# Transposing x as fp32 words that hold two bf16 each: four PE transposes a tile in place of eight

## The chip, the cores and the metric

The kernel runs on one core of a Trainium2 chip. The metric is the device time of one execution in microseconds (us), the median of repeated runs. PE is the tensor engine, PEld its weight loads, DVE the vector engine, ACT the scalar engine, POOL the GpSimd engine, SP the engine that issues the DMA transfers. A run has a state, fast or slow, judged by its time and its granted clock. On one chip the runs of the kernel before lie within 0.25% of each other. The kernel before had medians of 211.32, 211.36 and 211.38 us on three occasions and of 211.68 us on a fourth; the last three of these are on record for three different chips. So runs are compared with the kernel before of the same occasion.

## The reference

```python
batch, m, k, n = 16, 512, 1024, 768      # x: (16, 512, 1024), weight: (1024, 768), all float32
def reference(x, weight, bias, residual):
    return (np.matmul(x, weight) + bias + residual).astype(np.float32)
```

That is 8192 rows, in 64 tiles of 128. The kernel must read x (33.6 MB), the residual (25.2 MB) and the weight (3.1 MB) and write the output (25.2 MB): 87 MB.

## The kernel before

Rows are handled in groups of eight tiles (`J = 8`): one transfer brings x of a group, one its residual, one takes its output away. For each tile ACT casts x to bf16, PE transposes it into PSUM in eight pieces of 128x128, DVE copies these to SBUF, PE multiplies with the bf16 weight into PSUM, and DVE and POOL add residual and bias in place. Element pairs (2i, 2i+1) of a row of x share a place `i`: the weight is laid out to match (`w_d`), and each transpose takes the even or the odd elements of a block.

```python
n_c = K // (2 * P)                                              # 4 blocks of 256 elements
steps = [(c, e) for c in range(n_c) for e in range(2)]          # block, even or odd
w_d = weight.rearrange("(c p e) n -> p c e n", p=P, e=2)
# ... (loads, stores and rings of buffers cut: x_sb 2 groups, ro 4 groups, xb 4, xt 4, pt 2 tiles)
def cast(t, engine="act"):
    if t < n_t:
        xb[t] = ring(sb, "xb", t, 4, [P, n_c, P, 2], BF16)
        copy = nc.scalar.copy if engine == "act" else nc.vector.tensor_copy
        K_(copy(out=xb[t].rearrange("p c i e -> p (c i e)"), in_=x_sb[t // J][:, t % J, :]))

def transp(t):
    if t < n_t:
        pt = ring(ps, "pt", t, 2, [P, len(steps), P], BF16)
        for i, (c, e) in enumerate(steps):
            K_(nc.tensor.transpose(out=pt[:, i, :], in_=xb[t][:, c, :, e], identity=ident))
        xt[t] = ring(sb, "xt", t, 4, [P, len(steps), P], BF16)
        K_(nc.vector.tensor_copy(out=xt[t], in_=pt))

def mm(t, i, n0, nl):                                           # two chunks: 512 and 256 columns
    c, e = steps[i]
    K_(nc.tensor.matmul(po[t][:, n0:n0 + nl], lhsT=xt[t][:, i, :], rhs=w_sb[:, c, e, n0:n0 + nl],
                        start=(i == 0), stop=(i == len(steps) - 1)))
# ... (start cut)
for t in range(HEAD, n_t):
    cast(t + 2)
    S, j = divmod(t, J)
    if (t + 2) % J == J - 1:
        # ... (the first group's loads come in halves)
        load_x(S + X_BUFS)
        load_res(S + X_BUFS)
        if 1 <= S < n_s - 1:
            store(S - 1)
    if t < n_t - 1:
        for i in range(len(steps)):
            mms(t, i)                                           # both chunks of step i
            # ...
            if i == T_STEP:
                transp(t + 1)                                   # the next tile's transposes
    # ... (residual and bias, last stores)
```

## Time and profile before

| | kernel before |
|---|---|
| time, median | 211.28 us (211.23 to 211.34, the first three runs) |
| PE busy | 202.7 us, 97% of the profiled span of 210.0 us |
| one tile on PE, steady | 3.05 us: 16 output matmuls 2.60, 8 transposes 0.45 |
| moved by DMA | 87.27 MB |

From the page of the kernel before: the busy times, three of the rows in which the span is cut in 40 slices (tenths of busy time; the last is GB/s moved), and the chain of waits.

```profile
PE 202.7 (97%) x1555; PEld 131.7 (63%) x1555; DVE 104.9 (50%) x139; ACT 67.6 (32%) x68; POOL 115.1 (55%) x71
...
PE   7999999999999999999999999999999999999980
...
DMA  6999999999999999999999999999999999999993
GB/s 235 428 422 425 432 419 423 421 428 432 417 485 404 420 445 410 434 449 404 439 449 428 421 412 435 449 412 429 425 412 460 434 409 445 420 417 432 417 395 151
...
PE 96%; DVE 1%; issue 0%
PE po L101 79%; PE pt L95 14%; PE po L169 3%; PE po L189 1%; DVE xt L97 0%; DVE ro L128 0%; DVE warm L155 0%
```

Two things are full at once, PE and DMA, and the chain names only one of them.

The groups of instructions of the kernel before that the change touches (busy us, mean ns of one, idle time before them and what ended it):

```profile
L97 DVE COPY xt<-pt 128x1024 bf16<-128x1024 bf16 x64 | 44.1, 691 | 87.7 <-PE pt L95 87.5
...
L95 PEld LDWEIGHTS <-xb 128*128 128x128 bf16 x512 | 34.2, 99 | 8.8 <-DVE xb L87 0.7
L95 PE MATMUL pt<-ident,xb 128*128 128x128 bf16 x512 | 39.2, 220 | 0.0
```

The ends of matmuls are modelled, so 220 ns is not what one costs. What it costs is the distance between starts. The timeline of PE in the kernel before (start us, length us):

```profile
102.06 0.61 PE L95 MATMUL pt<-ident,xb 128*128 128x128 bf16 x8
102.51 2.76 PE L101 MATMUL po<-w_sb,xt 128*128 128x512 bf16 x16
105.11 0.39 PE L95 MATMUL pt<-ident,xb 128*128 128x128 bf16 x4
```

Eight transposes hold PE from 102.06 to 102.51, 0.45 us or 56 ns each, and sixteen output matmuls from 102.51 to 105.11, 2.60 us.

Stretches of the span of the kernel before (busy us and count of each engine, then the granted PE clock, the DMA share, GB/s):

```profile
20.00:60.00 40.00, 40.00 (x321) 26.51 (x319) 20.31 (x26) 13.88 (x15) 31.39 (x18) 1.00 1.01 424
...
100.00:140.00 40.00, 40.00 (x316) 26.42 (x315) 20.61 (x28) 13.92 (x14) 24.68 (x14) 1.00 1.01 432
```

PE does not wait at all, and the DMA share is at 1.01. The Trainium skill ("Perfetto Trace Analysis", Roofline) gives about 435 GB/s as what the 16 DMA engines of a core reach together; the trace agrees, with 424 to 432 GB/s at a full share over stretches of 40 us (single slices of the page swing from 395 to 485).

### The profile page before, as it was taken

Reading aid. Unit: us, or ns where it says so; the run is one execution under the profiler, and the core shown is the slowest. Engines: PE = TensorE matmul, PEld = TensorE weight load, DVE = VectorE, ACT = ScalarE, POOL = GpSimd, SP = SyncE. Lnnn points to the kernel's source line nnn. Section 1 sums busy time; section 2 is a strip of 40 time slices with the busy share of each in tenths; the row PEclk is TensorE's granted clock in tenths of the full one; section 3 lists DMA queues with packets and bytes.
Section 4 is the critical chain, followed back from the end, with each engine's and each line's share of the span. In section 5 each row is a group of like instructions: output and inputs, shape, how many; then the busy total and the mean of one; then the engine's idle time right before and its main releaser. Section 6 shows DMA issues by size and latency. Waiting matters only on the chain.

```text
span 210.0 us, 3632 instructions
## 1 busy us (share of the span) xinstructions
PE 202.7 (97%) x1555; PEld 131.7 (63%) x1555; DVE 104.9 (50%) x139; ACT 67.6 (32%) x68; POOL 115.1 (55%) x71
## 2 busy tenths in 40 slices
PE   7999999999999999999999999999999999999980
PEld 2666666666666666666666666666666666666650
DVE  0646464455445545544554455455445545545650
ACT  2543315331533063313432053230623116330000
POOL 2000097979999505991099703993039930799000
PEclk9999999999999999999999999999999999999998
DMA  6999999999999999999999999999999999999993
GB/s 235 428 422 425 432 419 423 421 428 432 417 485 404 420 445 410 434 449 404 439 449 428 421 412 435 449 412 429 425 412 460 434 409 445 420 417 432 417 395 151
DMA packets 6211, 87.27 MB, mean 416 GB/s; under 512 B 690, under 2 KB 818, under 8 KB 2099
## 3 DMA queue, kind: packets, MB, share of 16 engines
q1 hardware_dynamic: 6192, 87.03, 97.7%
q8 instruction: 12, 0.20, 0.4%
q14 instruction: 5, 0.03, 0.0%
q10 hardware_dynamic: 2, 0.00, 0.0%
HBM read 61.87 MB, written 25.17 MB: 415 GB/s over the span
## 4 chain that ended last, share of the span: by engine, by line
PE 96%; DVE 1%; issue 0%
PE po L101 79%; PE pt L95 14%; PE po L169 3%; PE po L189 1%; DVE xt L97 0%; DVE ro L128 0%; DVE warm L155 0%
## 5 line engine op out<-in xcount | busy, mean ns | idle before, releaser
L101 PE MATMUL po<-w_sb,xt 128*128 128x256 bf16 (+1 forms) x1024 | 176.7, 326 | 0.1
L101 PEld LDWEIGHTS <-xt 128*128 128x128 bf16 x1024 | 97.6, 98 | 58.8 <-DVE xt L97 0.5
L118 POOL TENSOR_TENSOR ro<-ro,bias_sb 128x768 f32<-128x768 f32 x52 | 92.4, 1813 | 51.7 <-DMA ro<-in_residual_dram 41.7
L87 ACT CAST xb<-x_tile 128x1024 bf16<-128x1024 f32 x62 | 62.8, 1044 | 115.5 <-DMA x_tile<-in_x_dram 54.2
L97 DVE COPY xt<-pt 128x1024 bf16<-128x1024 bf16 x64 | 44.1, 691 | 87.7 <-PE pt L95 87.5
L128 DVE TENSOR_TENSOR ro<-po,ro 128x768 f32<-128x768 f32 (+2 forms) x53 | 49.3, 933 | 2.9 <-PE po L101 2.8
L95 PEld LDWEIGHTS <-xb 128*128 128x128 bf16 x512 | 34.2, 99 | 8.8 <-DVE xb L87 0.7
L95 PE MATMUL pt<-ident,xb 128*128 128x128 bf16 x512 | 39.2, 220 | 0.0
L118 POOL TENSOR_TENSOR ro<-ro,tmp 128x768 f32<-128x768 f32 x12 | 21.5, 1815 | 26.6 <-DMA ro<-in_residual_dram 25.3
L126 DVE TENSOR_TENSOR tmp<-po,bias_sb 128x768 f32<-128x768 f32 x12 | 11.4, 948 | 0.9 <-POOL ro L118 0.5
L169 PE MATMUL po<-warm 128*128 128x512 bf16 x15 | 6.1, 581 | 1.2 <-DVE warm L155 1.2
L175 ACT CAST w_sb<-ro 128x768 bf16<-128x768 f32 x4 | 3.3, 832 | 4.0 <-DMA ro<-in_weight_dram 4.0
L169 PEld LDWEIGHTS <-warm 128*128 128x128 bf16 x15 | 1.9, 136 | 4.0 <-issue 2.7
L87 DVE CAST xb<-x_tile 128x1024 bf16<-128x1024 f32 x2 | 1.4, 693 | 4.9 <-DMA x_tile<-in_x_dram 4.9
L177 DVE CAST w_sb<-ro 128x768 bf16<-128x768 f32 x4 | 2.2, 554 | 2.2 <-DMA ro<-in_weight_dram 2.2
L160 ACT ACT_TABLE_LOAD x1 | 1.3, 1283 | 2.0 <-POOL ident masks.py:199 2.0
L189 PE MATMUL po<-tmp 128*128 128x512 f32 (+1 forms) x4 | 1.5, 500 | 0.0
L197 DVE COPY bias_sb<-po 128x768 f32<-128x768 f32 x1 | 1.0, 957 | 0.2 <-PE po L189 0.2
L189 PEld LDWEIGHTS po<-tmp 128*128 128x128 f32 x4 | 0.7, 190 | 0.5 <-issue 0.5
L132 POOL MEMSET tmp<- 128x768 f32 x1 | 0.7, 737 | 0.3 <-POOLq L266 0.3
L155 DVE MEMSET warm<- 128x256 uint32 x1 | 0.3, 272 | 0.9 <-PEq L266 0.9
masks.py:199 POOL TENSOR_SCALAR_AFFINE_SELECT ident<-ident 128x128 bf16<-128x128 bf16 x1 | 0.3, 292 | 0.1
(8 smaller groups left out, 1.0 us busy)
## 6 DMA issues: line engine op xcount, KB each, us to landing
out_dram<-ro SPq DMA_DIRECT2D x7, 3072.0 KB, 23.9
x_tile<-in_x_dram SPq DMA_DIRECT2D x5, 4096.0 KB, 30.5
ro<-in_residual_dram SPq DMA_DIRECT2D x5, 3072.0 KB, 17.8
ro<-in_residual_dram SPq DMA_DIRECT2D x6, 1536.0 KB, 27.4
x_tile<-in_x_dram SPq DMA_DIRECT2D x3, 2048.0 KB, 25.8
x_tile<-in_x_dram SPq DMA_DIRECT2D x5, 1024.0 KB, 18.5
ro<-in_weight_dram SPq DMA_DIRECT2D x4, 768.0 KB, 9.0
out_dram<-ro SPq DMA_DIRECT2D x1, 1536.0 KB, 11.6
```

The costliest lines, as they stand in the source:

```text
L87: K_(copy(out=xb[t].rearrange("p c i e -> p (c i e)"), in_=x_sb[t // J][:, t % J, :]))
L95: K_(nc.tensor.transpose(out=pt[:, i, :], in_=xb[t][:, c, :, e], identity=ident))
L97: K_(nc.vector.tensor_copy(out=xt[t], in_=pt))
L101: K_(nc.tensor.matmul(po[t][:, n0:n0 + nl], lhsT=xt[t][:, i, :], rhs=w_sb[:, c, e, n0:n0 + nl], start=(i == 0), stop=(i == len(steps) - 1),))
L118: K_(nc.gpsimd.tensor_add(out=r, in0=r, in1=tmp[t] if t < EARLY else bias_sb))
L126: K_(nc.vector.tensor_add(out=tmp[t], in0=p, in1=bias_sb))
L128: K_(nc.vector.tensor_add(out=row(t, n0, nl), in0=p, in1=row(t, n0, nl)))
L160: K_(nc.scalar.copy(out=warm_a, in_=warm_a))
L169: K_(nc.tensor.matmul(warm_ps[:, 0:512], lhsT=warm[:, 0:P], rhs=warm, start=True, stop=True))
L175: K_(nc.scalar.copy(out=w_sb[:, c, e, :], in_=w_st[:, c, e, :]))
L177: K_(nc.vector.tensor_copy(out=w_sb[:, c, e, :], in_=w_st[:, c, e, :]))
L189: K_(nc.tensor.matmul(bias_ps[:, n0:n0 + nl], lhsT=ones, rhs=bias_row[:, n0:n0 + nl], start=True, stop=True,))
```

## The change

Two neighbouring bf16 of a row are 32 bits. The change transposes them as one fp32 word: four transposes of 128 words in place of eight of 128 bf16, in the hope of fewer PE instructions. After the transpose a word still holds the even element and the odd one; the output matmuls pick theirs with a step of two when they load weights.

```diff
     def cast(t, engine="act"):
...
-            xb[t] = ring(sb, "xb", t, 4, [P, n_c, P, 2], BF16)
+            xb[t] = ring(sb, "xb", t, 4, [P, K], BF16)
...
     def transp(t):
         if t < n_t:
-            pt = ring(ps, "pt", t, 2, [P, len(steps), P], BF16)
-            for i, (c, e) in enumerate(steps):
-                K_(nc.tensor.transpose(out=pt[:, i, :], in_=xb[t][:, c, :, e], identity=ident))
-            xt[t] = ring(sb, "xt", t, 4, [P, len(steps), P], BF16)
+            pt = ring(ps, "pt", t, 2, [P, n_c, P], FP32)
+            pairs = xb[t][:, :].bitcast(FP32)
+            for c in range(n_c):
+                K_(nc.tensor.transpose(
+                    out=pt[:, c, :], in_=pairs[:, c * P:(c + 1) * P], identity=ident
+                ))
+            xt[t] = ring(sb, "xt", t, 4, [P, n_c, P], FP32)
             K_(nc.vector.tensor_copy(out=xt[t], in_=pt))
 
     def mm(t, i, n0, nl):
         c, e = steps[i]
+        both = xt[t][:, c, :].bitcast(BF16).rearrange("p (m e) -> p e m", e=2)
         K_(nc.tensor.matmul(
-            po[t][:, n0:n0 + nl], lhsT=xt[t][:, i, :], rhs=w_sb[:, c, e, n0:n0 + nl],
+            po[t][:, n0:n0 + nl], lhsT=both[:, e, :], rhs=w_sb[:, c, e, n0:n0 + nl],
...
-    ident = const.tile([P, P], BF16, name="ident")
+    ident = const.tile([P, P], FP32, name="ident")
```

More of the change, by code (lines that the diff above doesn't have):

```diff
@@ L84, in cast @@
         if t < n_t:
-            xb[t] = ring(sb, "xb", t, 4, [P, n_c, P, 2], BF16)
+            xb[t] = ring(sb, "xb", t, 4, [P, K], BF16)
             copy = nc.scalar.copy if engine == "act" else nc.vector.tensor_copy
-            K_(copy(
-                out=xb[t].rearrange("p c i e -> p (c i e)"), in_=x_sb[t // J][:, t % J, :]
-            ))
+            K_(copy(out=xb[t], in_=x_sb[t // J][:, t % J, :]))
     def transp(t):
         if t < n_t:
-            pt = ring(ps, "pt", t, 2, [P, len(steps), P], BF16)
-            for i, (c, e) in enumerate(steps):
-                K_(nc.tensor.transpose(out=pt[:, i, :], in_=xb[t][:, c, :, e], identity=ident))
-            xt[t] = ring(sb, "xt", t, 4, [P, len(steps), P], BF16)
+            pt = ring(ps, "pt", t, 2, [P, n_c, P], FP32)
[5 more added lines that the diff above has]
+            xt[t] = ring(sb, "xt", t, 4, [P, n_c, P], FP32)
             K_(nc.vector.tensor_copy(out=xt[t], in_=pt))
```

## The prediction

> **What bounds the kernel now.** Two things at once. The chain of waits is 96% PE: 79% output matmuls, 14% transposes of x. In the steady part a tile takes 3.05 us: sixteen matmuls 2.60 us, eight bf16 transposes 0.45 us (56 ns from start to start); PE never waits from 20 to 200 us (windows). But DMA is as full: share 1.00 to 1.01, at 424 to 432 GB/s, for 87.27 MB that the change does not touch. A group of eight tiles moves 10.5 MB in 24.4 us, which is 430 GB/s. The casts already find x late once per group (ACT waits 6.2 to 7.7 us for x); only the ring of four cast tiles hides that from PE.
>
> **What the change does.** Per tile, eight weight loads and matmuls of 128 bf16 columns become four of 128 fp32 columns. PSUM and xt bytes stay. The copy out of PSUM becomes 512 fp32 words in place of 1024 bf16 (0.69 us); fp32 additions out of PSUM took 691 ns at 512 columns, so I estimate 0.69 us again. The output matmuls load weights at a step of two elements; the transposes of before do that already, at 99 ns against 98 ns packed: no cost.
>
> **The uncertain term: one fp32 transpose.** The fp32 bias matmuls are the only sample: each is split in two instructions, and 768 columns took 1.35 us to the start of the next matmul: 1.76 ns a column, four times bf16. At that price four transposes take 0.90 us, and the kernel is 29 us slower. But the Trainium skill ("TensorE: Matmul & The Clock Gate", Terms) says that the transpose mode is 4x faster for FP32, so I expect one instruction at bf16's rate; no run here shows it. The weight load then matters: the same page (Fast Weight Load) excludes fp32 from the fast load. The trace agrees in direction: 190 ns for an fp32 load, 98 ns for bf16. I estimate 110 ns a transpose, load-bound: the 92 ns more, plus some 15 to 25 ns. Four take about 0.44 us against 0.45 now: PE gains almost nothing. If the loads hide, four take 0.23 us and PE is freed of 14 us.
>
> **Critical path.** Even then little shows, since DMA is full: only the tail (200 to 210 us: 2.57 MB, about 6 us of work at the full rate) can shrink, by 2 to 3 us; PE would wait for x at group starts instead. So halved transposes yield about 208 us, a neutral cost 210 to 211, 190 ns each (loads not hidden) about 231, four-fold columns 240.
>
> **Prediction: 210.4 us**, 8 in 10 between 207.5 and 216. Faster by over 2%: 4%; within 2%: 76%; slower by over 2%: 20%.
>
> **What would show each step.** Groups of instructions: 256 fp32 transposes, and the distance between two (110 ns expected; 56: loads hidden; 190 or more: wrong). Copy xt 0.69 us. Windows: output matmuls still 2.60 us a tile, DMA share still 1.00. If transposes got cheap, PE waits for casts, these for x, at group starts, and the span still ends at about 87 MB over 430 GB/s plus start and tail.
>
> **What would make it wrong.** fp32 transposes split into several passes; a switch cost between fp32 and bf16 on PE; strided loads of xt that slow the output matmuls (16 ns on each adds 16 us); or transfers faster than 430 GB/s once PE frees buffers earlier.

## The result

The changed kernel took 211.29 us (median of six runs, 211.19 to 211.48), the kernel before 211.32 us (six runs, 211.23 to 211.53): ratio 0.9998, 95% interval 0.9985 to 1.0011. A ratio here is the mean time of one kernel's fast runs over that of the other's of the same rounds, so it is not quite the ratio of the medians. The forecast was 210.4 us, 0.9 us (0.4%) less than before. The measured time lies inside the range that was given, but the gain did not come: the interval allows 0.3 us of it at most. The changed kernel's result is right.

From the page of the changed kernel:

```profile
PE 200.6 (96%) x1274; PEld 130.6 (62%) x1299; DVE 105.0 (50%) x139; ACT 67.6 (32%) x68; POOL 115.4 (55%) x71
...
PE   7999999999999999999999999999999999999980
...
DMA  6999999999999999999999999999999999999994
GB/s 237 427 425 427 429 416 428 418 441 419 432 457 440 408 423 426 444 419 435 432 429 435 427 419 446 437 426 423 418 435 437 457 405 416 441 433 430 408 404 155
...
PE 95%; issue 1%; DVE 1%
PE po L104 79%; PE pt L95 13%; PE po L172 3%; PE po L192 1%; DVE xt L99 0%; DVE ro L131 0%; DVE warm L158 0%
```

The two pages are almost the same (25 records of 512-column matmuls are missing from this trace: 1274 matmuls beside 1299 weight loads, so sums of PE are not compared). The groups:

```profile
L99 DVE COPY xt<-pt 128x512 f32<-128x512 f32 x64 | 44.2, 692 | 86.8 <-PE pt L95 86.6
...
L95 PE MATMUL pt<-ident,xb 128*128 128x128 f32 x256 | 38.3, 273 | 0.0
L95 PEld LDWEIGHTS pt<-ident,xb 128*128 128x128 f32 x256 | 29.8, 141 | 8.3 <-issue 0.8
```

The instructions are halved, 256 in place of 512. The copy takes 692 ns in place of 691. A weight load of a transpose takes 141 ns in place of 99. The timeline of PE in the changed kernel:

```profile
101.54 0.60 PE L95 MATMUL pt<-ident,xb 128*128 128x128 f32 x4
101.98 2.76 PE L104 MATMUL po<-w_sb,xt 128*128 128x512 bf16 x15
104.58 0.38 PE L95 MATMUL pt<-ident,xb 128*128 128x128 f32 x2
```

Four transposes hold PE for 0.44 us, 109 ns each ((0.60 - 0.273) / 3 from the first start to the fourth), where eight held it for 0.45. The output matmuls still take 2.60 us: the step of two costs nothing. Over 59 tiles, from the transposes at about 20 us to the last ones, a tile takes 3.037 us in place of 3.047. PE is 10 ns a tile faster, 0.6 us in all. Two questions stay: why an fp32 transpose costs just twice a bf16 one, and where the 0.6 us went.

```profile
20.00:60.00 40.00, 39.69 (x259) 26.32 (x263) 20.65 (x27) 14.06 (x16) 31.80 (x18) 1.00 1.01 426
...
100.00:140.00 40.00, 39.74 (x260) 26.30 (x264) 20.75 (x27) 13.95 (x14) 24.63 (x14) 1.00 1.01 431
```

The stretches of the changed kernel: DMA as full as before. The missing 0.3 us of PE are the missing records: in after_again, the same kernel profiled once more with no record missing, PE is busy for 40.00 of 40.00 us in both stretches.

### The profile page after: what moved, and what is told of

It is laid out like the page before. It is cut to its first block, busy times and chain, and to the rows that moved or that the text cites. A ratio compares the mean times of both kernels' runs of the same rounds, so it can differ in the third digit from the quotient of the medians.

```text
span 209.4 us, 3156 instructions
## 1 busy us (share of the span) xinstructions
PE 200.6 (96%) x1274; PEld 130.6 (62%) x1299; DVE 105.0 (50%) x139; ACT 67.6 (32%) x68; POOL 115.4 (55%) x71
## 4 chain that ended last, share of the span: by engine, by line
PE 95%; issue 1%; DVE 1%
PE po L104 79%; PE pt L95 13%; PE po L172 3%; PE po L192 1%; DVE xt L99 0%; DVE ro L131 0%; DVE warm L158 0%
## 5 line engine op out<-in xcount | busy, mean ns | idle before, releaser
L104 PE MATMUL po<-w_sb,xt 128*128 128x512 bf16 (+1 forms) x999 | 175.4, 324 | 1.4
L104 PEld LDWEIGHTS <-xt 128*128 128x128 bf16 x1024 | 100.1, 98 | 59.5 <-DVE xt L99 0.5
L99 DVE COPY xt<-pt 128x512 f32<-128x512 f32 x64 | 44.2, 692 | 86.8 <-PE pt L95 86.6
L95 PE MATMUL pt<-ident,xb 128*128 128x128 f32 x256 | 38.3, 273 | 0.0
L95 PEld LDWEIGHTS pt<-ident,xb 128*128 128x128 f32 x256 | 29.8, 141 | 8.3 <-issue 0.8
```

Source lines behind the costliest of these rows:

```text
L95: K_(nc.tensor.transpose(out=pt[:, c, :], in_=pairs[:, c * P:(c + 1) * P], identity=ident))
L104: K_(nc.tensor.matmul(po[t][:, n0:n0 + nl], lhsT=both[:, e, :], rhs=w_sb[:, c, e, n0:n0 + nl], start=(i == 0), stop=(i == len(steps) - 1),))
```

## The experiments

Two theories of the time. F: there is a floor, the time that the 87 MB of transfers take whatever PE does, and PE alone would need slightly less. P: PE sets the time, and its saving is only small. And two theories of the cost of an fp32 transpose. L (the one in the prediction): its weight load, which is slower for fp32. C: the streaming of its columns, at two cycles each in place of one.

| run | time, us | before, same occasion | ratio (95%) |
|---|---|---|---|
| half_tr | 211.31 | 211.36 | 0.9998 (0.9985 to 1.0010) |
| extra_tr | 212.82 | 211.36 | 1.0063 (1.0050 to 1.0076) |
| n64 | 211.55 | 211.36 | 1.0012 (0.9998 to 1.0025) |
| spread | 211.31 | 211.36 | 1.0002 (0.9989 to 1.0016) |
| before_hs | 209.14 | 211.68 | 0.9879 (0.9863 to 0.9896) |
| after_hs | 208.45 | 211.68 | 0.9850 (0.9835 to 0.9865) |
| half_hs | 196.47 | 211.68 | 0.9281 (0.9267 to 0.9295) |
| more_bytes | 222.91 | 211.68 | 1.0537 (1.0514 to 1.0561) |
| more_bytes2 | 219.65 | 211.38 | 1.0393 (1.0379 to 1.0407) |
| after_again | 211.25 | 211.38 | 0.9990 (0.9976 to 1.0003) |
| before_again | 211.42 | 211.38 | 0.9998 (0.9985 to 1.0010) |

### half_tr: half of the transposes left out of the kernel before

```diff
-            pt = ring(ps, "pt", t, 2, [P, len(steps), P], BF16)
-            for i, (c, e) in enumerate(steps):
-                K_(nc.tensor.transpose(out=pt[:, i, :], in_=xb[t][:, c, :, e], identity=ident))
-            xt[t] = ring(sb, "xt", t, 4, [P, len(steps), P], BF16)
+            pt = ring(ps, "pt", t, 2, [P, n_c, P], BF16)
+            for c in range(n_c):
+                K_(nc.tensor.transpose(out=pt[:, c, :], in_=xb[t][:, c, :, 0], identity=ident))
+            xt[t] = ring(sb, "xt", t, 4, [P, n_c, P], BF16)
...
-            po[t][:, n0:n0 + nl], lhsT=xt[t][:, i, :], ...
+            po[t][:, n0:n0 + nl], lhsT=xt[t][:, c, :], ...
```

> The kernel before with four of its eight bf16 transposes a tile left out (the odd elements are never transposed; the result is wrong on purpose, and the copy out of PSUM is half as long). It takes 4 x 56 ns x 64 = 14 us from PE and leaves every transfer as it was. Theory F (a floor of transfers: the 87 MB at about 430 GB/s, plus start and tail): 208 to 210 us, PE now waits for casts and these for x, DMA share stays 1.00. Theory P (PE alone sets the time): 211.3 - 14 = 197 us.

Measured: 211.31 us beside 211.36. Taking 14 us of work from PE moved nothing. Theory P is out. Theory F is right in kind, but the 208 to 210 us that it gave were too low: not even the tail shrank. The DMA share stays at 0.99 to 1.01 in every stretch from 20 to 200 us, so it is the transfers themselves that are full. PE now waits, as the waits of PE in half_tr show (us in total, times, longest):

```profile
PE pt L95 <- ACT xb L87: 6.9, 6, 2.8
```

PE waits for casts, and those for x (ACT waits 92.2 us for it in all, 54.2 in the kernel before). In the last 10 us of half_tr PE has nothing left to do (its busy time is the second figure), and the transfers still run as in the kernel before:

```profile
200.00:202.00 2.00, 0.00 (x0) 0.00 (x0) 0.00 (x0) 0.00 (x0) 0.00 (x0) 1.00 0.98 415
202.00:204.00 2.00, 0.00 (x0) 0.00 (x0) 0.00 (x0) 0.00 (x0) 0.00 (x0) 0.88 0.96 393
204.00:206.00 2.00, 0.00 (x0) 0.00 (x0) 0.00 (x0) 0.00 (x0) 0.00 (x0) 0.50 0.86 336
206.00:208.00 2.00, 0.00 (x0) 0.00 (x0) 0.00 (x0) 0.00 (x0) 0.00 (x0) 0.50 0.26 97
208.00:210.00 2.00, 0.00 (x0) 0.00 (x0) 0.00 (x0) 0.00 (x0) 0.00 (x0) 0.50 0.00 0
```

And the same stretches of before_again, the kernel before unedited (its last matmuls start just before 204 us):

```profile
200.00:202.00 2.00, 2.00 (x13) 1.13 (x12) 1.32 (x2) 0.00 (x0) 0.00 (x0) 1.00 0.97 409
202.00:204.00 2.00, 1.81 (x13) 0.99 (x11) 1.12 (x3) 0.00 (x0) 0.00 (x0) 1.00 0.95 390
204.00:206.00 2.00, 0.00 (x0) 0.00 (x0) 0.27 (x1) 0.00 (x0) 0.00 (x0) 1.00 0.87 342
206.00:208.00 2.00, 0.00 (x0) 0.00 (x0) 0.00 (x0) 0.00 (x0) 0.00 (x0) 0.79 0.36 136
208.00:210.00 2.00, 0.00 (x0) 0.00 (x0) 0.00 (x0) 0.00 (x0) 0.00 (x0) 0.50 0.00 2
```

The share of DMA falls off in much the same way in both, from about 205 us on, though half_tr had issued its last store at 200.2 us: stores that were queued before still drain. After 208 us half_tr moves nothing, and its span ends at 209.4; these last 1.4 us belong to the floor too. Why the share falls off before the queue is empty was not tested. The chain of half_tr names transfers where that of the kernel before named PE:

```profile
DMA 78%; PE 12%; SPq 2%; ACT 1%; issue 1%; DVE 0%; ACTq 0%
```

### extra_tr: the first transpose of each tile made twice

```diff
                 K_(nc.tensor.transpose(out=pt[:, i, :], in_=xb[t][:, c, :, e], identity=ident))
+                if i == 0:
+                    K_(nc.tensor.transpose(out=pt[:, i, :], in_=xb[t][:, c, :, e], identity=ident))
```

> The kernel before with the first bf16 transpose of each tile made twice (the result stays right): 56 ns x 64 = 3.6 us more on PE, transfers as before. If PE still sets the pace at all: 214.9 us. If only the transfers do and PE had slack: under 213 us.

Measured: 212.82 us, 1.5 us more than before for 3.6 us of PE work (a tile went from 3.05 to 3.10 us in the trace). So I estimate that PE of the kernel before had about 2.1 us to spare below the floor (3.6 - 1.5). This is the second case named, at its edge.

### n64: fp32 transposes that load 128 columns but stream 64

```diff
-            pt = ring(ps, "pt", t, 2, [P, n_c, P], FP32)
+            pt = ring(ps, "pt", t, 2, [P, n_c, P // 2], FP32)
...
-                    out=pt[:, c, :], in_=pairs[:, c * P:(c + 1) * P], identity=ident
+                    out=pt[:, c, :], in_=pairs[0:P // 2, c * P:(c + 1) * P], identity=ident[0:P // 2, 0:P // 2]
...                                                       # xt likewise half as long; lhsT = its 128 bf16
```

> The changed kernel with fp32 transposes that load the same 128 columns of weights but stream only 64 columns (64 partitions of the tile alone; the result is wrong on purpose). Theory L (a transpose costs its fp32 weight load): still about 109 ns from start to start, time as the changed kernel. Theory C (the streamed fp32 columns set it, two cycles a column): about 55 ns, four take 0.22 us.

Measured, in the timeline of PE of n64:

```profile
102.77 0.46 PE L95 MATMUL pt<-ident,xb 64*128 64x64 f32 x4
103.16 2.78 PE L104 MATMUL po<-w_sb,xt 128*128 128x512 bf16 x16
105.86 0.46 PE L95 MATMUL pt<-ident,xb 64*128 64x64 f32 x4
```

The merged line hides that the four starts are not evenly spaced. The same view with its window ended after the second and after the third start (`--window 102.7:102.9` and `102.7:102.95`):

```profile
102.77 0.33 PE L95 MATMUL pt<-ident,xb 64*128 64x64 f32 x2
102.77 0.40 PE L95 MATMUL pt<-ident,xb 64*128 64x64 f32 x3
```

The later transposes last 221 to 223 ns each by the model. Taken off the ends, that puts the second start 0.11 us after the first, and the third and the fourth 0.06 to 0.07 us after the one before. The start times of the trace, to the nanosecond, have about 112, 62 and 61 ns in nearly every tile, and then 152 ns to the first output matmul. So 64 columns cost 62 ns in a row, near the 55 of C and far from the 109 of L. The loads of this trace (64 partitions, 128 columns of fp32, 138 ns each) follow each other at that pace, so a load of 138 ns does not have to cost 109. The experiment is unclean all the same: the trace lists these transposes as 64*128, where all others are 128*128, and a tile takes 3.09 us, longer than with full transposes. The extra time lies where the shape changes: the 256-column matmul just before the transposes holds PE for 202 ns in place of 109, the first transpose for 112 in place of 62, and the last for 152. The output matmuls come to 2.70 us in place of 2.60. The Trainium skill ("TensorEngine Tiling (Array Packing)", Key Properties) says that a change of tiling mode drains PE; these numbers fit that, but no run here tests it alone.

### spread: the four fp32 transposes set between output matmuls

```diff
         for n0, nl in chunks:
             mm(t, i, n0, nl)
+            if n0 == 0 and between:
+                between()                     # transpose number i of tile t + 1, for i < 4
...
-                if i == T_STEP:
-                    transp(t + 1)
```

> The changed kernel with its four transposes of a tile not in a row but one after each of the first four 512-column matmuls, so that their weight loads can run under these (the result stays right). Theory L: each then costs about 56 ns on PE, a tile takes 2.82 us in place of 3.04 where it does not wait for x, and the time is 208 to 210 us, held by the transfers (theory F), or 197 (theory P). Theory C: still 109 ns each, and the time stays within 0.5 us of the changed kernel.

Measured, in the timeline of spread:

```profile
102.41 0.14 PEld L96 LDWEIGHTS pt<-ident,xb 128*128 128x128 f32 x1
102.62 0.27 PE L96 MATMUL pt<-ident,xb 128*128 128x128 f32 x1
102.62 0.21 PEld L110 LDWEIGHTS <-xt 128*128 128x128 bf16 x2
102.73 0.49 PE L110 MATMUL po<-w_sb,xt 128*128 128x256 bf16 x2
```

The weight load of the transpose ran from 102.41 to 102.55, under a 512-column matmul, and was over 0.07 us before the transpose started at 102.62. Still the next matmul starts 0.11 us later. Nor is it the bf16 load that follows: after the last bf16 transpose of the kernel before, the same kind of load and matmul follow, and the matmul starts 56 ns after the transpose. The load is hidden and the cost is the same: theory L is out. Nor is it a cost of changing between fp32 and bf16: spread goes from bf16 to fp32 four times a tile and the changed kernel once, and both take 3.037 us a tile.

C holds, and the first profile of the kernel before says the same, which was overlooked when the prediction was made. The fp32 bias matmuls are split in two instructions for each of the two chunks, four in all. The last two weight loads begin as the second instruction of 512 columns and the first of 256 start:

```profile
8.60 1.51 PE L189 MATMUL po<-tmp 128*128 128x512 f32 x4
9.09 0.19 PEld L189 LDWEIGHTS po<-tmp 128*128 128x128 f32 x1 [0.24 <-issue]
9.52 0.19 PEld L189 LDWEIGHTS po<-tmp 128*128 128x128 f32 x1 [0.24 <-issue]
9.95 2.76 PE L101 MATMUL po<-w_sb,xt 128*128 128x512 bf16 x16
```

From 9.09 to 9.52 runs the second instruction of 512 columns (429 ns by the exact starts), and from 9.52 to 9.95 run two of 256 columns (216 ns each). That is 0.84 ns a column for one fp32 instruction, as the transposes cost at 128 columns (109 ns). Two cycles at 2.4 GHz (the clock that the Trainium skill gives in "TensorE: Matmul & The Clock Gate", Part 1; the granted clock was 1.00 in the stretches above) for 128 columns are 107 ns. The same page (Back-to-back issue gap) adds about 2.5 ns to a matmul on its own. With it the estimate is 109 ns for 128 fp32 columns and 56 ns for 128 bf16 columns, both as measured. For a stream of weight loads and matmuls, which this is, the page gives 81 ns at 128 columns; that isn't what was measured here. Four fp32 transposes and eight bf16 ones stream for the same number of cycles; what the change saves is four times that small fixed part, by this estimate some 10 ns a tile, as measured. The 62 ns of n64, where two cycles a column would give 56, are not fully explained.

### before_hs, after_hs and half_hs: the same kernels with less to write

In the kernel before, the changed kernel and half_tr, six of the big stores write half of their columns:

```diff
             if 1 <= S < n_s - 1:
-                store(S - 1)
+                store(S - 1, 0, J, 0, N // 2)
```

> The kernel before with six of its big stores cut to half of their columns (9.4 MB less to write, about 22 us of transfers; result incomplete on purpose). PE has the same work. With transfers no longer full, PE alone should set the time: PE ends at 204 us as before, its last stores land without a queue, so 209 to 210.5 us. If transfers alone set the time before: about 190.

> The changed kernel with the same six stores cut. If four fp32 transposes save only 9 ns a tile (two cycles a column, as runs spread and n64 suggest), and PE sets the time here: 0.6 us less than before_hs, in every round. If the missing gain of the change were something on PE or DVE and not the floor of transfers: equal to before_hs.

> The kernel with half of its bf16 transposes (wrong result on purpose), with the same six stores cut. With the floor of transfers gone, the 14 us of PE that were worth nothing in half_tr should now show: 195 to 197 us. If something other than the transfers held half_tr: equal to before_hs.

Measured: 209.14, 208.45 and 196.47 us, all as expected. With the floor out of the way, the kernel before takes 2.5 us less than with all its stores (0.9879). That is the time that PE sets, and it fits with the 2.1 us to spare in extra_tr, within 0.4 us (two occasions, on two chips). The changed kernel with cut stores is 0.69 us faster than the kernel before with cut stores: here the 0.6 us that PE saves show. And half of the transposes are worth 12.7 us (14 us of PE, less 1.2 us in which PE of half_hs waits for casts). One line of a profile would have told the two cases apart (transfers last, or PE last): the landing of the last store of 128 KB (the last figure, us from issue to landing). In the kernel before:

```profile
out_dram<-ro SPq DMA_DIRECT2D x1, 128.0 KB, 4.3
```

In half_tr, where it is issued 5 us earlier (SP's last issue ends at 200.2 us in place of 205.2) and takes 5 us longer:

```profile
out_dram<-ro SPq DMA_DIRECT2D x1, 128.0 KB, 9.1
```

In before_hs, with no queue ahead of it:

```profile
out_dram<-ro SPq DMA_DIRECT2D x1, 128.0 KB, 1.9
```

The 2.4 us between 4.3 and 1.9 are the queue that the last store of the kernel before found, about what PE had to spare.

### more_bytes and more_bytes2: 3.1 MB more to write

```diff
+                if S == 3:
+                    store(S - 1)                          # more_bytes: the same store again
```

> The kernel before with one 3.1 MB store made twice (same data, result right), 7.3 us more of transfers at 430 GB/s, nothing more on any engine. Floor of transfers: 218.6 us, less by up to 1 us if the tail overlaps better. If PE sets the time: 211.3.

Measured: 222.91 us, 11.2 more, where 7.3 were expected. The second store had to wait for the first one to land (SP waited 23.4 us there), and so the loads behind it came late and DMA ran dry, as a stretch of more_bytes shows (second figure from the right):

```profile
135.00:140.00 5.00, 4.95 (x42) 3.34 (x41) 2.22 (x4) 1.66 (x2) 5.00 (x4) 1.00 0.59 251
```

So it added bytes and a wait. Mended, with bytes that nothing waits for:

```diff
+            if S == 3:
+                for jj in range(J):
+                    K_(nc.sync.dma_start(out=out_d[5, :, jj, :], in_=bias_sb))
```

> more_bytes mended: the extra 3.1 MB come from a constant tile and go to rows that a later store overwrites (the result stays right), so that no buffer and no second store waits for them. Floor of transfers: 3.1 MB at 430 GB/s, 7.3 us more, 218.6 us, and PE waits for casts that wait for x. PE alone: 211.3 us. If the 11.2 us of more_bytes were the price of the bytes and not of the wait for the first store: 222.5.

Measured: 219.65 us, 8.3 more (0.0393 of 211.38), with no more work on any engine. Theory P's 211.3 is out here too; theory F's 7.3 is 1 us short. These bytes go in eight transfers of rows of 3 KB, with 1152 more packets in all than before; that they are less efficient would explain it, but it was not tested.

### after_again and before_again

Both unedited, on one chip.

> The changed kernel once more, unedited, beside the next run on the same chip. Floor of transfers: within 0.3 us of before, though a tile takes 9 ns less on PE. If the 0.6 us that PE saves come through at all: 0.4 to 0.7 us less than before.

> The kernel before once more, unedited, as a null: ratio 1 within 0.15%; and a second profile of it, to see whether its span of 210.0 us in the first profile was long by chance (the changed kernel's runs had 209.4 to 209.7): expected 209.5, with the last matmul at 204 us.

Measured: ratio 0.9990 (0.9976 to 1.0003) for the changed kernel, 0.9998 for the kernel before against itself; spans of 209.2 to 209.5 and 209.3 to 209.8 us. The first profile of the kernel before, with 210.0 us, was a long one by chance, so its 0.6 us against the changed kernel's 209.4 were not the gain. The interval of after_again alone would leave room for 0.5 us of gain; that of the result above leaves 0.3 at most. Both kernels are on the floor.

No experiment pointed to a version that beats both: with every byte written, no cut on PE went below 211.3 us.

## Why the prediction was right or wrong

- That PE and DMA are both full, and that cheaper transposes would hardly show: right. half_tr is within 0.15% of the kernel before with 14 us less on PE.
- The step that failed is "only the tail ... can shrink, by 2 to 3 us", and with it the 0.9 us that the forecast took off the time. It counted the end as room: 2.57 MB in 10 us, at the full rate 6 us. half_tr showed a tail of nearly the same form when PE had ended 5 us earlier. Stores issued before are still queued; from about 205 us DMA falls off, so that the last transfer ends at about 208 us and not at 206; then 1.4 us without transfers follow. That term measured 0 in place of 2 to 3 us. The prediction does not say how the 210.4 us were put together. Its 210 to 211 us for transposes of the same cost as before lie below the 211.3 measured before, so it seems that the 0.6 us of PE were counted as gained in the time too. PE had 2.1 to 2.5 us to spare already before the change (extra_tr, before_hs), so any gain of PE only adds to what is spare.
- The saving on PE was sized right, 0.44 us for four transposes against 0.45, and after_hs shows it in the time, 0.69 us, once the floor is lowered. The reason given was wrong. The prediction called the fp32 transpose bound by its weight load (theory L); it streams at two cycles a column (spread, n64, the bias matmuls), and the agreement of 110 ns with 109 was luck. The case "If the loads hide, four take 0.23 us" cannot come: they are hidden in spread, and it costs the same. The sample that the prediction had, 1.76 ns a column for fp32 in two instructions, is 0.88 ns for each; one instruction at that price is 113 ns for 128 columns, close to the right number for the right reason.
- The chance of several passes, at four times the bf16 cost a column, did not come true: one instruction each, at twice the cost. The copy (692 ns) and the stepped weight loads (98 ns, output matmuls 2.60 us) were right.

## What to carry to other kernels

Where two resources are full at once, the chain of waits may name only one: it named PE for 96% here, and 14 us less of PE changed nothing. Ask what each would take alone: add a little work to one, and take load off the other, before trusting a gain that lies on the chain. Packing two bf16 into an fp32 word halved the instructions of the PE transposes here (256 in place of 512), but not their time (0.44 us a tile in place of 0.45), so it was worth 10 ns a tile.

## What the Trainium skill lacked or had wrong

- "TensorE: Matmul & The Clock Gate", Terms: the transpose mode is called 4x faster for FP32, without saying than what. Here an fp32 transpose costs 109 ns for 128 columns, 0.85 ns a column, where the fp32 bias matmuls cost 1.76 ns a column: about 2x faster than these, as one instruction is faster than two, and twice the cost of a bf16 transpose.
- The same page, Part 4: it has times only for a bf16 transpose (about 390 ns in isolation and 275 ns in a kernel), and none for fp32. In a row, the distance from start to start was 56 ns for bf16 and 109 ns for fp32; the modelled durations were 220 and 273 ns.
- The same page, Fast Weight Load: it excludes fp32, and the trace agrees (141 ns against 99). But it does not say whether the slower load costs time: in spread it was over 0.07 us before its matmul, and in n64 fp32 loads followed each other every 62 ns.
- "Perfetto Trace Analysis", Roofline: the 435 GB/s ceiling is confirmed (424 to 432 GB/s for 180 us). That page does not say how the rate falls off at the end of a program: here DMA fell off from about 205 us, had nothing from about 208, and the span ended at 209.4 to 209.6 us, in half_tr (PE done at 199 us) as in before_again (PE done at 204 us).
